# A decoder trunk with 31 instead of 28 slots for split weights, and 1 KB of descriptor region

## The chip, the core and the metric

The kernel runs on one core of a Trainium2 chip. TensorE (PE in the profile) multiplies, VectorE (DVE) and ScalarE (ACT) do elementwise work and copy results out of PSUM, GpSimd (POOL) does a few small operations, and SyncE (SP) issues the transfers between HBM and the on-chip memory SBUF. The metric is the device time of one execution in microseconds (us). Each engine takes its instructions in the order in which they stand in its program.

## What is computed

The reference is a decoder of four layers over 256 positions of width 1024, all in float32. Cut to its frame:

```python
def reference(x, ...):
    for i in range(DEPTH):                       # DEPTH = 4
        g = norm_g[i]
        x = x + 0.5 * rms_norm(swiglu(rms_norm(x, g[0]), ffn_w_in[i, 0], ffn_w_out[i, 0]), g[1])
        hm = rms_norm(x, g[2])
        # i % 3: 0 sliding_sink_attention, 1 nsa_attention, 2 moba_attention
        x = x + rms_norm(m, g[3])
        x = x + 0.5 * rms_norm(swiglu(rms_norm(x, g[4]), ffn_w_in[i, 1], ffn_w_out[i, 1]), g[5])
    return x
```

`swiglu` multiplies by a 1024 x 5632 and a 2816 x 1024 matrix; there are eight of them. The mixers of layers 0 and 3 attend to a window of 128 keys (called A below), that of layer 1 adds three branches with gates, one of them over compressed keys (B), and that of layer 2 is plain causal attention at this length (C).

## The kernel before

The 256 positions are two chains of 128 rows (`Chain`, t = 0 and 1), which pass through the same stages; at each step a recording layer takes the chain or side job that its own clock holds to be ready first (`choose`), so that one chain's matmuls fill the time in which the other's softmax or norm runs. What it takes is written into TensorE's program in that order, and the instructions of the other engines go into their programs as they come.

Weights come as 313 slabs of 128 x 2048 in two halves each, 625 halves in all (one slab is short). A half of 512 KB is loaded into one of four `raw` tiles, then split in two: ScalarE copies it to `hi` (rounded), VectorE subtracts to get `lo`. Both are tiles of 4 KB a partition in the pool `p4`, tag `k4`. Activations are split likewise into `xh` and `xl` (in the FFN's second product `hh` and `hl`), and each product is three matmuls: hi by xh, lo by xh, hi by xl. All matmul operands of this kind are 128 x 512; the groups of a half step (four contraction blocks) are 12 matmuls, called a proj group below.

The pool also holds the attention's keys (`kT`, `vs`, `cT`), queries, scores of chain 1, outputs `o`, and the compression's operands: everything that is 4 KB. How far the splitting runs ahead of TensorE is set by the free slots. Lines 366 and 387 count them:

```python
def room():
    return (SLOTS - 2 * (plan.split - plan.freed)
            - sum(max(h, w) for h, w in zip(plan.held, plan.want)))
...
        if plan.split < len(halves) and (urgent or clock.now >= plan.at + PACE) and room() >= 2:
            hi = p4.tile([P, HALF], F32R, tag="k4", name="hi")
            lo = p4.tile([P, HALF], F32R, tag="k4", name="lo")
```

`plan.freed` counts halves that both chains have used. So with 28 slots and nothing else held, 14 halves (seven slabs) are split at most. Where a `hi` stands in ScalarE's program is decided by this count and by the clock of the recording layer: it stands behind whatever was recorded before it, such as `h` (the gate of the FFN, read from a `proj` result) or `hh` (the copy of a transposed `h`).

In the setup, two of these slots hold a table for the position bias (`setup`, matmul `tab`), until it is written to `scratch`. In mixer B a side job (`compress`) adds position vectors to transposed keys (DVE `k<-k,post`, eight instructions), multiplies them (`hid`) and goes on to compressed keys and values, beside the two chains' scores (`acc<-k,k`), softmax, transposes (`trp`) and products with the values (`pv`). Transposes of keys and queries are `trq`.

Of the kernel before, what the change touches and what calls it, by code (L numbers as in the profile page):

```python
# [35 lines left out]

REP = 32
GATE_SLAB = 112
SLOTS = 28
NP2 = 6  # L40
NRAW = 4
NPP = 4
# [218 lines left out]
def trunk(ctx: ExitStack, tc: tile.TileContext, x, rel, gains, pre, sinks, pos, w1, w2, wts, hot,  # L261
# [5 lines left out]
    def pool(name, bufs, **kw):  # L267
        return ctx.enter_context(tc.tile_pool(name=name, bufs=bufs, **kw))

    const = pool("const", 1)  # L270
    praw = pool("praw", NRAW)
    p4 = pool("p4", SLOTS)
    p2 = pool("p2", NP2)
# [22 lines left out]
# [4 lines that stand above are left out]
    def k4(who, shape, dtype=F32):  # L300
        plan.held[who] += 1
        assert sum(plan.held) + 2 * (plan.split - plan.freed) <= SLOTS
        return p4.tile(shape, dtype, tag="k4", name="k4")
# [820 lines left out]
```

## Time and profile before

| | |
|---|---|
| median of 3 runs | 1977.15 us (1976.63 to 1980.09) |
| the profiled execution | 1981.12 us, its span 1979.3 us |
| TensorE busy | 1938.0 us, 98% of the span |
| VectorE, ScalarE busy | 1234.2 us (62%), 1039.2 us (53%) |
| mean granted clock of TensorE | 0.994 |

The span runs from the first to the last instruction; 1.8 us of the profiled execution lie outside it. Its time is 3.97 us above the median of the runs, within their spread. Busy times are unions of an engine's instructions; the ends of matmuls are modelled, so a matmul of 0.39 us that starts 0.23 us after the one before it overlaps it.

### The profile page before, as it was taken

The page shows a single profiled execution, that of the slowest core. Times are in us where ns is not written, and L with a number is a line of the kernel's source. Part 1 is how long each engine was busy: PE and PEld are TensorE (multiplying, and loading weights), DVE is VectorE, ACT ScalarE, POOL GpSimd, SP SyncE. Part 2 cuts the span into 40 slices and gives each one's busy share as a digit, 9 for nine tenths or more (in the row PEclk, how much of TensorE's full clock was granted, in tenths as well). Part 3 has the DMA queues.
Part 4 walks back from the last instruction along what each step waited for, and adds up shares of the span by engine and source line. Part 5 has one row for each costly group of instructions (what it writes and reads, how often), then busy time and mean ns, then how long its engine had stood idle before and what let it go on. Part 6 is the DMA issues. An engine that isn't in the chain of part 4 may idle for free.

```text
span 1979.3 us, 27414 instructions
## 1 busy us (share of the span) xinstructions
PE 1938.0 (98%) x9978; PEld 1586.7 (80%) x9978; DVE 1234.2 (62%) x2267; ACT 1039.2 (53%) x1885; POOL 43.0 (2%) x62
## 2 busy tenths in 40 slices
PE   7999999999999998999999999999999999999998
PEld 6778878888888876788888888778888888878887
DVE  6566666556655648765576556566557655676554
ACT  6345655445544546554455455655445544665442
POOL 0000000000000000000000000000000000000000
PEclk9999999999999999999999999999999999999999
DMA  8758556555556454465556555655555555436551
GB/s 271 210 192 241 176 137 200 190 185 186 195 188 193 153 165 116 139 202 188 185 170 209 185 185 175 188 148 196 185 189 181 195 188 191 161 112 205 185 186 58
DMA packets 114131, 356.42 MB, mean 180 GB/s; under 512 B 12843, under 2 KB 30507, under 8 KB 113996
## 3 DMA queue, kind: packets, MB, share of 16 engines
q1 hardware_dynamic: 113996, 354.68, 55.4%
q8 instruction: 78, 1.28, 0.3%
q14 instruction: 57, 0.47, 0.1%
HBM read 352.01 MB, written 2.62 MB: 179 GB/s over the span
## 4 chain that ended last, share of the span: by engine, by line
PE 90%; ACT 3%; DVE 3%; DMA 2%; issue 1%; SPq 0%; POOL 0%; DVEq 0%; POOLq 0%; ACTq 0%
PE proj L228 56%; PE acc L228 29%; ACT k L210 2%; PE trh L235 2%; DVE k L210 2%; DMA raw<-wts 1%; PE trx L235 1%; DVE lo L210 1%; PE pv L228 1%; DMA bias<-scratch 1%; PE trp L235 1%; ACT hi L210 1%; DVE pT L210 0%; PE trq L235 0%; ACT xh L210 0%
## 5 line engine op out<-in xcount | busy, mean ns | idle before, releaser
L210 DVE TENSOR_TENSOR lo<-raw,hi 128x1024 fp32r<-128x1024 f32 x625 | 760.3, 1223 | 371.3 <-ACT hi L210 338.7
L210 ACT ACTIVATE hi<-raw 128x1024 fp32r<-128x1024 f32 x625 | 659.3, 1063 | 369.3 <-PE acc L228 187.5
L228 PE MATMUL proj<-hi,xh 128*128 128x512 f32 (+1 forms) x1696 | 673.9, 398 | 2.7 <-DVE xl L210 1.7
L228 PE MATMUL proj<-lo,xh 128*128 128x512 f32 (+1 forms) x1696 | 657.4, 389 | 0.8 <-DVE lo L210 0.8
L228 PE MATMUL proj<-hi,xl 128*128 128x512 f32 (+1 forms) x1696 | 448.6, 387 | 0.0
L228 PEld LDWEIGHTS proj<-hi,xh 128*128 128x128 f32 x1696 | 320.0, 189 | 64.0 <-ACT xh L210 2.8
L228 PEld LDWEIGHTS proj<-lo,xh 128*128 128x128 f32 x1696 | 320.4, 189 | 61.4 <-DVE lo L210 1.1
L228 PEld LDWEIGHTS proj<-hi,xl 128*128 128x128 f32 x1696 | 315.6, 188 | 67.3
L228 PE MATMUL acc<-hi,hh 128*128 128x512 f32 x704 | 223.7, 392 | 3.1 <-ACT hh L210 3.1
L228 PE MATMUL acc<-lo,hh 128*128 128x512 f32 x704 | 222.2, 389 | 0.0
L228 PE MATMUL acc<-hi,hl 128*128 128x512 f32 x704 | 191.3, 390 | 0.0
L210 ACT ACTIVATE h<-proj,rh 128x256 f32<-128x256 f32 x176 | 81.9, 465 | 182.3 <-PE proj L228 180.8
L210 ACT ACTIVATE hh<-trh 128x256 fp32r<-128x256 f32 x176 | 67.0, 380 | 180.8 <-PE trh L235 180.7
L228 PEld LDWEIGHTS acc<-hi,hh 128*128 128x128 f32 x704 | 130.9, 188 | 30.2 <-ACT hh L210 3.9
L228 PEld LDWEIGHTS acc<-hi,hl 128*128 128x128 f32 x704 | 132.1, 188 | 27.7
L228 PEld LDWEIGHTS acc<-lo,hh 128*128 128x128 f32 x704 | 132.1, 188 | 27.6
L210 DVE SCALAR_TENSOR_TENSOR h<-h,proj 128x256 f32<-128x256 f32 x176 | 73.6, 418 | 116.2 <-ACT h L210 116.1
L210 DVE TENSOR_TENSOR hl<-trh,hh 128x256 fp32r<-128x256 f32 x176 | 73.9, 420 | 113.2 <-ACT hh L210 113.1
L210 DVE SCALAR_TENSOR_TENSOR h<-proj,c,h 128x256 f32<-128x256 f32 x176 | 85.0, 483 | 5.1
L210 ACT ACTIVATE k<-k,nm 128x128 f32<-128x128 f32 (+1 forms) x160 | 70.7, 445 | 32.0 <-DVE nm L210 32.0
L210 POOL TENSOR_TENSOR r<-v,mhalf 128x1 f32<-128x1 f32 x48 | 36.0, 750 | 1818.4 <-DVE v L210 1818.4
L235 PE MATMUL trh<-ident,h 128*128 128x128 f32 x352 | 67.0, 272 | 0.0
(99 smaller groups left out, 1133.4 us busy)
## 6 DMA issues: line engine op xcount, KB each, us to landing
raw<-wts SPq DMA_DIRECT2D x624, 512.0 KB, 4.6
bias<-scratch SPq DMA_DIRECT2D x96, 128.0 KB, 4.6
g<-gains SPq DMA_DIRECT2D x12, 512.0 KB, 4.8
k<-w SPq DMA_DIRECT2D x8, 512.0 KB, 8.3
scratch<-k SPq DMA_DIRECT2D x4, 384.0 KB, 6.6
out<-x SPq DMA_DIRECT2D x4, 256.0 KB, 2.0
x<-x SPq DMA_DIRECT2D x2, 256.0 KB, 3.0
x<-x SPq DMA_DIRECT2D x1, 512.0 KB, 7.2
```

Of the source, the lines that this page charges most:

```text
L210: return call(out, *args, **kw)
L228: self.engine.matmul(out, lhs, rhs, **kw)
L235: self.engine.transpose(out, src, ident)
```

## The change

Two constants. The pool of 4 KB tiles gets three slots more, 12 KB a partition, and the region that is set aside at the start of SBUF for descriptors of dynamic DMAs is set to 1024 bytes a partition; without the argument it has 16384.

```diff
-SLOTS = 28
+SLOTS = 31
@@ kernel()
-    nc = bacc.Bacc("TRN2", target_bir_lowering=False, num_devices=1)
+    nc = bacc.Bacc("TRN2", target_bir_lowering=False, num_devices=1,
+                   dynamic_dma_scratch_size=1024)
```

`SLOTS` also stands in `room()`, so the recording layer records splits earlier (with nothing else held 15 halves instead of 14), and since its clock decides by when a weight is ready, some instructions change places on every engine. The number of matmuls, 9262, stays. On TensorE all but some ten places read alike in both programs. Three places follow; numbers behind names tell tiles apart and are shifted between the two programs.

ScalarE, in the first FFN of layer 0, where the setup's two slots are held. Before, at the place where four splits follow an `h` that reads the finished `proj_900`:

```order
L210 ACTIVATE h_896<-proj_839,rh_257 128x256
L210 ACTIVATE hh_940<-trh_937 128x256
L210 ACTIVATE h_957<-proj_900,rh_290 128x256
L210 ACTIVATE hi_913<-raw_831 128x1024
L210 ACTIVATE hi_919<-raw_837 128x1024
L210 ACTIVATE hi_961<-raw_868 128x1024
```

Now, one block later (this place has splits ahead of its `hh` and `h` now):

```order
L210 ACTIVATE hh_1080<-trh_1077 128x256
L210 ACTIVATE h_1096<-proj_1040,rh_290 128x256
L210 ACTIVATE hi_1004<-raw_923 128x1024
L210 ACTIVATE hi_1010<-raw_929 128x1024
L210 ACTIVATE hi_1053<-raw_971 128x1024
...
L210 ACTIVATE hh_1218<-trh_1215 128x256
L210 ACTIVATE hi_1125<-raw_1057 128x1024
L210 ACTIVATE h_1234<-proj_1178,rh_290 128x256
L210 ACTIVATE hi_1143<-raw_1063 128x1024
```

So the burst of splits that stands behind an `h` has moved by one block of the FFN, and a second one follows: `hi_1143` stands behind `h_1234`.

TensorE at these places. Before, four matmuls stand between the end of `proj_900` and the first use of `hi_913`:

```order
L228 MATMUL proj_900<-hi_675,xl_231 128x512
L228 MATMUL proj_973<-hi_870,xh_126 128x512
L228 MATMUL proj_973<-lo_871,xh_126 128x512
L228 MATMUL proj_973<-hi_870,xh_128 128x512
L228 MATMUL proj_973<-lo_871,xh_128 128x512
L228 MATMUL proj_973<-hi_913,xh_130 128x512
L228 MATMUL proj_973<-lo_914,xh_130 128x512
```

Now none stands between `proj_1040` and `hi_1004`; at the second place there are again four, between `proj_1178` and `hi_1143`:

```order
L228 MATMUL proj_1040<-hi_772,xl_231 128x512
L228 MATMUL proj_1112<-hi_1004,xh_126 128x512
L228 MATMUL proj_1112<-lo_1005,xh_126 128x512
...
L228 MATMUL proj_1178<-hi_925,xl_231 128x512
L228 MATMUL proj_1250<-hi_1125,xh_126 128x512
L228 MATMUL proj_1250<-lo_1126,xh_126 128x512
L228 MATMUL proj_1250<-hi_1125,xh_128 128x512
L228 MATMUL proj_1250<-lo_1126,xh_128 128x512
L228 MATMUL proj_1250<-hi_1143,xh_130 128x512
L228 MATMUL proj_1250<-lo_1144,xh_130 128x512
```

TensorE where mixer B goes over from projections to scores. Before, ten transposes, three proj groups (cut here to the last matmul of one), four transposes, and then the first scores of chain 0 and of chain 1:

```order
L235 MATMUL trq_6562<-ident_94,k2_6493 128x128 x4
L235 MATMUL trq_6568<-ident_94,k2_6495 128x128 x4
L235 MATMUL trq_6574<-ident_94,k2_6547 128x128 x2
...
L228 MATMUL proj_6578<-hi_6556,xl_6242 128x512
L235 MATMUL trq_6674<-ident_94,k2_6638 128x128 x2
L235 MATMUL trq_6692<-ident_94,k2_6659 128x128 x2
L228 MATMUL acc_6685<-k4_6065,k4_6067 128x128 x2
L228 MATMUL acc_6686<-k4_6065,k4_6067 128x128 x2
L228 MATMUL acc_6703<-k4_6065,k4_6256 128x256 x2
L228 MATMUL acc_6704<-k4_6065,k4_6256 128x256 x2
```

Now the first proj group stands ahead of the transposes, the first scores of chain 0 right behind them, then two proj groups, and then three more groups of scores before `hid`:

```order
L235 MATMUL trq_6619<-ident_94,k2_6574 128x128 x2
L228 MATMUL acc_6600<-k4_6071,k4_6073 128x128 x2
L228 MATMUL acc_6601<-k4_6071,k4_6073 128x128 x2
...
L228 MATMUL proj_6640<-hi_6528,xl_6248 128x512
L228 MATMUL acc_6600<-k4_6071,k4_6073 128x128 x2
L228 MATMUL acc_6601<-k4_6071,k4_6073 128x128 x2
L235 MATMUL trp_6731<-ident_94,k2_6627 128x128 x2
L235 MATMUL trp_6736<-ident_94,k2_6627 128x128 x2
L235 MATMUL trq_6752<-ident_94,k2_6700 128x128 x2
L228 MATMUL acc_6763<-k4_6071,k4_6275 128x256 x2
L228 MATMUL acc_6764<-k4_6071,k4_6275 128x256 x2
```

So the first scores of chain 0 have moved ahead of two proj groups, and the transposes behind one. On VectorE the order there was: eight `post` additions, three `lo`, scores of chain 0, scores of chain 1. It is now: one `post`, the first scores of chain 0, seven `post`, two `lo`, the second scores of chain 0, one `lo`, the first scores of chain 1.

## Rows read from the trace of the kernel before

**Rows 1.** The page's head and its first part: busy us of each engine.
```profile
span 1979.3 us, 27414 instructions
PE 1938.0 (98%) x9978; PEld 1586.7 (80%) x9978; DVE 1234.2 (62%) x2267; ACT 1039.2 (53%) x1885; POOL 43.0 (2%) x62
```

**Rows 2.** Busy us by stretches of 100 us, then granted clock, DMA share.
```profile
0.00:100.00 100.00, 88.60 (x390) 71.39 (x391) 59.45 (x94) 51.48 (x79) 1.81 (x8) 1.00 0.76 238
...
500.00:600.00 100.00, 100.00 (x452) 82.26 (x451) 59.98 (x74) 48.08 (x61) 0.00 (x0) 1.00 0.60 199
...
700.00:800.00 100.00, 89.64 (x909) 70.89 (x907) 72.28 (x278) 59.95 (x184) 5.23 (x7) 0.97 0.45 138
```

**Rows 3.** Waits of PE over the span: us, times, longest.
```profile
PE trx L235 <- DMA x<-x: 8.4, 2, 4.7
PE acc L228 <- DVE mx L210: 5.4, 8, 1.6
...
PE proj L228 <- DVE lo L210: 0.8, 1, 0.8
...
PE proj L228 <- ACT hi L210: 0.6, 1, 0.6
```

**Rows 4.** Timeline of PE around 103 us: start, length, instruction, idle before.
```profile
102.04 0.39 PE L228 MATMUL proj<-hi,xh 128*128 128x512 f32 x1
...
102.72 0.39 PE L228 MATMUL proj<-lo,xh 128*128 128x512 f32 x1
103.72 0.50 PE L228 MATMUL proj<-hi,xh 128*128 128x512 f32 x1 [0.60 <-ACT hi L210]
104.98 0.50 PE L228 MATMUL proj<-lo,xh 128*128 128x512 f32 x1 [0.76 <-DVE lo L210]
```

**Rows 5.** Timeline of ACT, the same place.
```profile
102.24 0.47 ACT L210 ACTIVATE h<-proj,rh 128x256 f32<-128x256 f32 x1 [2.37 <-PE proj L228]
102.61 3.89 ACT L210 ACTIVATE hi<-raw 128x1024 fp32r<-128x1024 f32 x4
```

**Rows 6.** Busy us in three parts of mixer B, columns as in rows 2.
```profile
724.00:734.00 10.00, 9.49 (x43) 7.36 (x42) 9.29 (x10) 5.90 (x12) 0.00 (x0) 1.00 0.55 199
734.00:784.00 50.00, 41.58 (x538) 32.10 (x537) 42.78 (x210) 31.01 (x120) 3.78 (x5) 0.97 0.49 149
784.00:803.00 19.00, 17.42 (x232) 12.62 (x231) 15.49 (x57) 11.80 (x37) 2.56 (x3) 1.00 0.31 84
```

**Rows 7.** Timeline of PE at the start of mixer B's scores.
```profile
723.02 1.59 PE L235 MATMUL trq<-ident,k 128*128 128x128 f32 x10
...
733.68 0.44 PE L235 MATMUL trq<-ident,k 128*128 128x128 f32 x2 [0.35 <-ACT k L210]
...
739.26 0.72 PE L228 MATMUL acc<-k,k 64*128 64x128 f32 x8
739.91 0.66 PE L235 MATMUL trp<-ident,k 128*128 128x128 f32 x4
742.22 2.00 PE L228 MATMUL acc<-k,k 64*128 64x128 f32 x16 [1.65 <-DVE mx L210]
...
760.12 1.14 PE L228 MATMUL acc<-k,k 64*128 64x256 f32 x8
```

**Rows 8.** Timeline of DVE, the same place.
```profile
724.63 7.73 DVE L210 TENSOR_TENSOR k<-k,post 64x480 f32<-64x480 f32 x8 [4.68 <-ACT k L210]
732.39 3.50 DVE L210 TENSOR_TENSOR lo<-raw,hi 128x1024 fp32r<-128x1024 f32 x3
735.81 0.28 DVE L210 CUSTOM_DVE_ANT_0 k<-acc,bias 128x128 f32<-128x128 f32 x1
736.02 0.08 DVE L210 DVE_READ_ACCUMULATOR2_ANT mx<- 128x1 f32 x1
```

**Rows 9.** The page's DMA queue and its issues of weights: packets, MB; us to landing.
```profile
q1 hardware_dynamic: 113996, 354.68, 55.4%
...
raw<-wts SPq DMA_DIRECT2D x624, 512.0 KB, 4.6
```

## The prediction

> **What bounds the kernel now.** I read the page's busy times first, then the same by stretches, then TensorE's waits, and then timelines at the two places where the order of instructions changes. TensorE is busy for 1938.0 of 1979.3 us [rows 1], so all of its idle time is 41.3 us. The stretches show where that lies: in the FFNs there is none (100.00 of 100 us, at the full granted clock), in the first 100 us there are 11.4 us, in the stretch with mixer B 10.4 us [rows 2]. Of the first, 8.4 us are the wait for x itself [rows 3], which no slot touches. Two things follow. Splitting weights further ahead can give nothing inside the FFNs, where TensorE never waits. And a gain can only come from the places where TensorE starves: the setup and the mixers. Waits that name a weight (`lo` or `hi`) make 1.4 us in the whole run [rows 3]; the rest of the mixers' waits name the softmax, and there more weights help only if they let matmuls of a projection be put into the gaps.
>
> **The change part by part.** First the region of descriptors. All weight loads are issued from SyncE's queue, and the 113,996 packets of the run went through one queue that the page calls hardware_dynamic [rows 9]. No row shows the region used or not used, so its price is bounded from both sides. From below nothing: a transfer that doesn't read its descriptors there doesn't see its size. From above by the landing times: a weight load takes 4.6 us to land and four can be under way, so one lands every 1.15 us, while 625 halves in 1979.3 us are one every 3.17 us; a smaller region costs nothing until it makes a landing more than 2.7 times as long (12.7 us). I take nothing. The Trainium skill (DMA: Bandwidth & Descriptors, section "SWDGE vs HWDGE vs iDMA") says that the rings in SBUF belong to transfers that GpSimd issues and that those issued from SyncE or ScalarE never touch that path; by it the price is nothing as well, whatever the size, and no run before this one has a smaller region to show it.
>
> Then the three slots. They add no instruction: as many halves, matmuls and transfers as before. What changes is the order, at few places, so the cost is the sum over these.
>
> *The FFNs.* A split stands one half earlier there, and on ScalarE bursts of two and two become one and three. TensorE doesn't wait there and the order of its matmuls is the same, so the price is nothing as long as `hh` isn't held up. Its cover is a proj group: twelve matmuls at 0.227 us (102.04 to 102.72 is three of them [rows 4]) are 2.72 us. A burst of three is at most one split more ahead of an `hh`, 3.89 / 4 = 0.97 us [rows 5], less than the cover. If it were gone, eight FFNs of eleven blocks would each pay up to that, 85 us; nothing in the rows points to it.
>
> *The setup, around 103 us.* This is the place that I hold to be decisive. The setup's table takes two slots, no split is recorded for a while, and when they come they stand behind an `h` on ScalarE, which can't start before a `proj` is complete. Before, the rows show what this costs: `h` starts at 102.24, four `hi` follow from 102.61, and TensorE, which would have gone on at 102.72 + 0.23 = 102.95, starts at 103.72 with the first `hi`, 0.77 us late; its next matmul needs `lo`, starts at 104.98 instead of 103.95, and is 1.03 us late [rows 4, 5]. Sum 1.80 us, with four matmuls (102.04 to 102.72) between the end of `proj` and the first use of the new `hi`. In the changed program this place has its splits earlier, so the 1.80 us go. But one block later the same thing stands with no matmul between: TensorE would go on at the place of 102.04 and starts at that of 103.72, 1.68 us late, and 1.03 us for `lo` again, 2.71 us. And a block after that it stands once more with four matmuls between, as before: 1.80 us. So 4.51 us take the place of 1.80 us, a loss of 2.7 us. Behind the waiting matmul on TensorE everything waits; nothing makes it up, since the FFNs behind it run without a gap. From below this term is 0 (the splits could have run ahead by then for a reason that I don't see, such as a clock that is late on both sides), from above 4.5 us, if the old wait stayed too. I take 2.7 us.
>
> *Mixer B, 723 to 803 us.* Before, TensorE waits 0.35 and 1.65 us up to 742.22 [rows 7], and from 734 to 784 it is idle for 50 - 41.58 = 8.4 us in all [rows 6]. VectorE is the tighter engine there: busy 9.29 of 10 us from 724, and 42.78 of 50 us from 734 [rows 6]. In the changed program chain 0's first scores stand two proj groups ahead (5.44 us), which gives its softmax matmuls to hide behind. But the transposes that feed `compress` stand a proj group later, so VectorE's eight `post` additions start later. I go through the first part by rows. Transposes began at 723.02 and `post` at 724.63, 1.61 us behind [rows 7, 8]. Now the transposes begin at 723.02 + 2.72 = 725.74, two others stand ahead of those that matter (2 of 10 in 1.59 us, 0.3 us), so `post` starts at 727.65. VectorE then has eight `post` (7.73 us), the four score operations (0.21 us each from 735.81 to 736.02, 0.84 us), two `lo` of the three that took 3.50 us (2.33 us), to 738.6, and two score operations of the second job before the first PSUM bank is free: 739.0. TensorE: twelve transposes (1.9 us) to 727.65, scores 0.65 us (739.26 to 739.91), two proj groups 5.44, scores 0.65, four transposes 0.6, two more 0.3, scores over 256 keys 1.1 us (760.12), which is 736.4. It then needs that bank: a wait of 2.6 us. Before, the same part held 2.0 us of waits, so this is a loss of 0.6 us. At that point VectorE has done the same jobs in both programs, the remaining work is the same, and from 784 on the order of TensorE is the same again. What the middle, 744 to 784, does with its waits of 8.4 - 0.35 - 1.65 = 6.4 us is the open part: from below all of it goes (-6.4), from above VectorE's later start of 727.65 - 724.63 = 3.0 us is nowhere regained (+3.0). I take nothing for it, since VectorE's work there is the same and its share of 86% leaves little to shift.
>
> *Mixers A and C and the end.* In A the order of TensorE is the same; in C sixteen `pv` move behind the first products of the output projection, in the last A four transposes; each has matmuls of its own to stand beside. Nothing, give or take 0.6 us for the sixteen `pv` if the scores behind them are late.
>
> Sum: 2.7 + 0.6 = 3.3 us. The profiled execution took 1981.12 us and would take 1984.4; it is 3.97 us above the median of the runs, 1977.15 us, and against that the time is **1980.5 us**.
>
> **The rivals.** *The gaps of B are filled.* The earlier scores let the softmax of chain 0 run under proj groups, and the waits of 744 to 784 go, 6.4 us, with the 0.6 us of the first part not lost: 1977.15 + 2.7 - 6.4 = 1973.5 us, and with the old 2.0 us of the first part gone too, 1971.5 us. For it speaks that the waits there are many small ones; against it that VectorE is busy for 86% of that time and gets no work taken away. It ends as faster from a gain in B of 6.7 us on. *VectorE's late start in B is kept to the end.* Since `post` starts 3.0 us later and VectorE is nearly full behind it, all that follows is 3.0 us late: 1977.15 + 2.7 + 3.0 = 1982.9 us. For it speaks 9.29 of 10 us; against it 7.2 us of idle VectorE in the 50 us behind. It ends as slower where more than 1.3 us of the 3.0 stay. *The setup costs nothing.* The splits are on time, and the slots do what they do elsewhere, nothing: 1977.15 + 0.6 = 1977.8 us. The rows of 103 us speak against it. *The region throttles the loads.* With 1 KB for what had 16 KB, loads that could only go one at a time would land every 4.6 us, 625 of them in 2875 us; only a landing rate under one in 3.17 us decides. The single hardware queue speaks against it.
>
> **How the numbers follow.** A difference of 0.2%, 3.95 us, is about what a measurement of this kernel can tell from no change (the three runs spread over 3.46 us), so faster is below 1973.2 and slower above 1981.1 us. The forecast has a chance of 0.47, and its own terms move it by some 1.5 us to either side, so a fifth of it, 0.1, lies above 1981.1 us. The setup at no cost has 0.12 (same). B filled has 0.18, of which 0.12 get past 1973.2 us. B late has 0.22, of which 0.20 get past 1981.1 us. The throttled region has 0.01. That makes slower 0.31, same 0.57, faster 0.12. The range leaves out a tenth at each end: from 1974.0, inside B filled, to 1983.0, just above B late.
>
> **What the profile after would show.** TensorE's waits on `hi` and `lo` in the first 130 us: 0.60 and 0.76 us at 103 us should be gone, and in their place two pairs, about 1.7 and 1.0 us near 118 us and 0.8 and 1.0 us some 20 us later. In B the `post` additions should start 3 us later than before in relation to the last projections, with a wait of TensorE on `mx` of 2 to 3 us right ahead of `hid`. The FFNs should stay at 100.00 of 100 us. The landing of weights should stay near 4.6 us. I am wrong if the pairs in the setup don't appear, if the idle time in B changes by more than 3 us, or if any FFN shows waits.

## The result, and the profile after

The changed kernel took 1994.96 us (median of 4 runs, 1990.96 to 1997.79), the kernel before 1977.72 us (4 runs). The ratio is 1.0084, with an interval from 1.0064 to 1.0104. So it is slower, by 17 us in this comparison, and the prediction (1980.5 us, at most 1983.0) was wrong. Two later comparisons of the same two kernels, with 11 and 35 and with 11 and 31 runs, gave 1.0029 [1.0013, 1.0045] and 1.0034 [1.0016, 1.0052]: slower as well, by 6 to 7 us. Why the sizes differ is told below. One later run of each kernel took 9 and 15% longer, at a granted clock of 0.85 and 0.80, and is in no figure here.

The page of the changed kernel answers to [rows 1, 9]:

```profile
span 1993.9 us, 27323 instructions
...
PE 1942.3 (97%) x9978; PEld 1586.2 (80%) x9978; DVE 1230.1 (62%) x2267; ACT 1017.2 (51%) x1885; POOL 41.6 (2%) x62
...
q1 hardware_dynamic: 113996, 354.68, 56.2%
...
raw<-wts SPq DMA_DIRECT2D x624, 512.0 KB, 4.7
```

TensorE's idle time has grown from 41.3 to 51.6 us and its busy time by 4.3 us, though no matmul was added. Of the latter, 1.7 us are stretches at a lower clock (10.2 us were lost in them before, 11.9 us now, summed over windows of 5 us); the rest stays open. TensorE's waits over the span, against [rows 3]:

```profile
PE trx L235 <- DMA x<-x: 9.4, 2, 5.9
PE trx L235 <- DVE x L210: 7.2, 7, 2.2
PE acc L228 <- DVE mx L210: 6.9, 8, 2.9
PE acc L228 <- ACT hh L210: 3.7, 3, 2.5
PE proj L228 <- ACT hi L210: 2.1, 2, 1.5
...
PE pv L228 <- DVE v L210: 1.7, 1, 1.7
...
PE proj L228 <- DVE lo L210: 1.5, 2, 0.8
```

The row to see is the second. `trx` are the transposes of a chain's new x behind its norm, at the end of an FFN or mixer. Before they waited for x twice and 2.4 us, now seven times and 7.2 us. Of the 2.4 us, most is one wait behind the first mixer A,

```profile
273.61 1.94 PE L235 MATMUL trx<-ident,x 128*128 128x128 f32 x8 [1.98 <-DVE x L210]
```

which is 0.57 us now; without it the waits for x went from 0.4 to 6.6 us. The interior of the FFNs is as it was, 100.00 of 100 us, and the first 100 us have lost 2 us more than in [rows 2]:

```profile
0.00:100.00 100.00, 86.61 (x380) 69.89 (x381) 60.32 (x94) 52.03 (x79) 1.80 (x8) 1.00 0.77 241
500.00:600.00 100.00, 100.00 (x455) 82.35 (x453) 61.10 (x83) 47.38 (x68) 0.22 (x1) 1.00 0.60 192
```

**Where the time went.** I laid the two traces side by side at each `trx` and read how the distance grows. To the first: 1.0 us, the load of x, which another profile of the old order has too. In the first FFN with the setup: 6.4 us, of which 2.2 us are longer waits for `hi` and `lo` and 1.7 us a stretch at lower clock. In the first mixer A: -2.65 us, since 1.4 us of the wait just shown and a stretch at lower clock (0.85 at 270 and 0.81 at 275 us before) are missing. At the FFNs' later ends: 7.4 us in all, at most 2.2 us at one. In mixer B: -1.7 us, in C 0.3 us. In the last A: 3.8 us. The sum is 14.5 us.

**The end of an FFN.** ScalarE there, before and now (first the kernel before):

```profile
1003.05 1.06 ACT L210 ACTIVATE hi<-raw 128x1024 fp32r<-128x1024 f32 x1 [1.92 <-DMA raw<-wts]
1004.32 1.06 ACT L210 ACTIVATE hi<-raw 128x1024 fp32r<-128x1024 f32 x1 [0.21 <-DMA raw<-wts]
1005.29 0.58 ACT L210 ACTIVATE junk<-acc 128x512 bf16<-128x512 f32 x1
...
1006.03 0.60 ACT L210 ACTIVATE junk<-acc 128x512 bf16<-128x512 f32 x1
```

```profile
1008.70 1.06 ACT L210 ACTIVATE hi<-raw 128x1024 fp32r<-128x1024 f32 x1 [1.99 <-DMA raw<-wts]
1009.66 0.58 ACT L210 ACTIVATE junk<-acc 128x512 bf16<-128x512 f32 x1
...
1012.47 1.06 ACT L210 ACTIVATE hi<-raw 128x1024 fp32r<-128x1024 f32 x1 [2.14 <-DMA raw<-wts]
1013.44 0.58 ACT L210 ACTIVATE junk<-acc 128x512 bf16<-128x512 f32 x1
```

The two `junk` are the sums of squares of the two halves of the FFN's result; the norm, x and the next transposes wait for both. Now a `hi` stands between them, and it waits for its own load. VectorE and TensorE of the changed kernel show the rest of the chain:

```profile
1014.14 0.16 DVE L210 SCALAR_TENSOR_TENSOR v<-ss,v 128x1 f32<-128x1 f32 x1 [2.46 <-ACT junk L210]
...
1014.96 1.42 DVE L210 SCALAR_TENSOR_TENSOR x<-k,r,x 128x512 f32<-128x512 f32 x2
```

```profile
1015.86 1.23 PE L235 MATMUL trx<-ident,x 128*128 128x128 f32 x8 [2.23 <-DVE x L210]
```

That `hi` was recorded behind the `junk` (tiles are numbered as they are recorded) and still stands ahead of the second one, because the order in the programs of ScalarE, VectorE and SyncE isn't that of the recording: the compiler moves instructions against each other. The section on the kernel said otherwise (a `hi` "stands behind whatever was recorded before it"). ScalarE's program at this norm in the changed kernel:

```
L210 ACTIVATE junk_99,ss_9442<-acc_7958 128x512
L210 ACTIVATE hi_9479<-raw_9397 128x1024
L210 ACTIVATE junk_99,ss_9442<-acc_7959 128x512
```

In the program before, where the same `hi` stands behind both, the norms of an FFN's or mixer's result have a `hi` between their two `junk` at 8 places, all of chain 1; now at 16. Seven of the eight new places are in chain 0.

**Why there.** A slab of two halves gives its four slots back in the order lo, lo, hi, hi, as TensorE is done with them, and new halves take slots in the order in which they come free. By the slots in the compiled programs, with 28 slots 272 of the 625 halves take two former `lo` and 270 two former `hi`. With 31 the row is shifted by one: 269 take a former `lo` for their `hi` and a former `hi` for their `lo`, and 267 take the last `hi` of one slab for their `hi` and the first `lo` of the next for their `lo`. Every second `lo` therefore waits until the next slab is in use, and so does the load into the raw tile that this `lo` sets free. VectorE's waits, first before, then now:

```profile
DVE lo L210 <- ACT hi L210: 338.7, 337, 12.1
...
DVE lo L210 <- PE acc L228: 7.6, 3, 4.4
```

```profile
DVE lo L210 <- ACT hi L210: 178.7, 206, 12.1
...
DVE lo L210 <- PE acc L228: 87.6, 65, 2.3
...
DVE lo L210 <- PE trh L235: 41.3, 58, 0.8
```

`lo` behind its own `hi` became `lo` behind TensorE, 123 times. That an odd number of slots does this was the first theory ("pairs"); its rivals were the changed order of TensorE, which comes with the higher count in `room()` ("order"), and the descriptor region.

### The profile page after: what moved, and what is told of

It reads as the page before. It is cut to its first block, busy times and chain, and to the rows that moved or that the text cites. A ratio compares the mean times of both kernels' runs of the same rounds, so it can differ in the third digit from the quotient of the medians.

```text
span 1993.9 us, 27323 instructions
## 1 busy us (share of the span) xinstructions
PE 1942.3 (97%) x9978; PEld 1586.2 (80%) x9978; DVE 1230.1 (62%) x2267; ACT 1017.2 (51%) x1885; POOL 41.6 (2%) x62
## 4 chain that ended last, share of the span: by engine, by line
PE 85%; DMA 5%; DVE 5%; ACT 4%; issue 2%; POOL 0%; SPq 0%; DVEq 0%; POOLq 0%; ACTq 0%
PE proj L228 53%; PE acc L228 27%; DMA raw<-wts 4%; ACT k L210 2%; PE trh L235 2%; DVE k L210 2%; DVE lo L210 1%; PE trx L235 1%; ACT hi L210 1%; DMA bias<-scratch 1%; PE pv L228 1%; ACT junk L210 1%; DVE x L210 0%; PE trp L235 0%; DVE pT L210 0%
## 5 line engine op out<-in xcount | busy, mean ns | idle before, releaser
L210 ACT ACTIVATE hi<-raw 128x1024 fp32r<-128x1024 f32 x625 | 646.2, 1060 | 479.7 <-PE acc L228 192.5
```

The source lines that it names most:

```text
L210: return call(out, *args, **kw)
```

## The experiments

In the table, "counted" is the number that `room()` works with, "slots" that of the pool. The kernel before was run beside each four on the same chip: medians 1982.33, 1982.72, 1982.83 and 1982.04 us. Each run is listed with its mean granted clock, and time times clock, called the product here, is an estimate of what the run would have taken at full clock: the waits are in it, what a lower clock costs is not. It is the sharper measure: the runs of before (126) have a standard deviation of 3.1 to 4.0 us in time and of 1.4 to 1.6 us in this product, whose means on the four chips are 1972.0, 1971.7, 1971.9 and 1971.4. The last column is the mean product against that of before on the same chip; its standard error is 0.4 to 0.9 us.

| run | slots, counted | median us | ratio, interval | mean clock | product |
|---|---|---|---|---|---|
| e1_region | 28, 28 | 1983.63 | 0.9993 [0.998, 1.0007] | 0.9951 | 0.0 |
| e2_31_counted_28 | 31, 28 | 1987.48 | 1.003 [1.0016, 1.0043] | 0.9947 | +5.8 |
| e3_30 | 30, 30 | 1990.29 | 1.0039 [1.0025, 1.0052] | 0.9938 | +5.7 |
| e4_29 | 29, 29 | 1987.51 | 1.0039 [1.0019, 1.0059] | 0.9964 | +10.5 |
| e5_32_counted_31 | 32, 31 | 1987.31 | 1.0023 [1.0011, 1.0035] | 0.9948 | +5.6 |
| e6_setup_28 | 32, 28 in the setup | 1983.44 | 1.0005 [0.9991, 1.0018] | 0.9953 | +2.0 |
| e7_end_28 | 32, 28 in layer 3 | 1987.04 | 1.0023 [1.0012, 1.0033] | 0.9938 | +3.3 |
| e8_mid_31 | 32, 28 in both | 1980.38 | 0.9986 [0.9975, 0.9996] | 0.9958 | +0.2 |
| e9_31_again | 31, 31 | 1988.90 | 1.0029 [1.0013, 1.0045] | 0.9950 | +7.1 |
| e10_31_junk_first | 31, 31 | 1984.01 | 1.0005 [0.999, 1.002] | 0.9949 | +1.8 |
| e11_31_counted_28_junk_first | 31, 28 | 1983.71 | 1.0002 [0.9987, 1.0017] | 0.9934 | -1.1 |
| e12_mid_31_junk_first | 32, 28 in both | 1982.79 | 1.0008 [0.9991, 1.0025] | 0.9940 | -0.5 |
| e13_set_31 | 32, 31 in the setup | 1991.92 | 1.0058 [1.0037, 1.0079] | 0.9930 | +7.6 |
| e14_end_31 | 32, 31 in layer 3 | 1988.26 | 1.0031 [1.0016, 1.0047] | 0.9949 | +6.0 |
| e15_32_counted_28 | 32, 28 | 1983.25 | 1.0004 [0.9988, 1.0021] | 0.9951 | +2.8 |
| e16_31_third | 31, 31 | 1988.96 | 1.0034 [1.0016, 1.0052] | 0.9955 | +8.6 |

All of them have the 1 KB region.

**Region, odd pool, order (e1 to e4).** The edits, against the changed kernel: `SLOTS` is 28, 30 or 29 in e1, e3 and e4; e2 is

```diff
-SLOTS = 31
+SLOTS, COUNT = 31, 28
-        return (SLOTS - 2 * (plan.split - plan.freed)
+        return (COUNT - 2 * (plan.split - plan.freed)
-        assert sum(plan.held) + 2 * (plan.split - plan.freed) <= SLOTS
+        assert sum(plan.held) + 2 * (plan.split - plan.freed) <= COUNT
```

e1: 

> 28 slots as before, and only the descriptor region is 1 KB; every engine has the order of before. Region theory (the smaller region slows transfers): all or most of the loss is here, about 1995 us, and the landing of weights is the 4.7 us of the changed kernel or more. Pairs theory (an odd number of slots parts hi and lo of one half) and order theory (the recording layer's earlier splits change the order): no difference, 1977.7 us, ratio between 0.998 and 1.002.

e2: 

> The pool has 31 slots, but the recording layer counts 28, so TensorE's order is that of before to the last instruction; only the order on ScalarE, VectorE and SyncE changes. Pairs theory: a hi still stands between the two junk of chain 0's norms, so the loss at the ends of the FFNs (about 7.4 us) and that of the last mixer A (about 4 us) stay and only the setup's part goes: about 1989 us, with trx waiting for x some seven times. Order theory: nothing in TensorE's order has changed, so 1977.7 us and two waits for x as before.

e3: 

> 30 slots, counted as 30: an even number, with two of the three slots more and a changed order of TensorE. Pairs theory: hi and lo stay together, no hi between the two junk of chain 0, trx waits for x twice as before, and what is left is the setup's order: 1977.7 to 1981 us. Order theory: two thirds of the loss of 17 us, about 1989 us.

e4: 

> 29 slots, counted as 29: an odd number, with one of the three slots more, and TensorE's order nearly that of before. Pairs theory: hi and lo are parted, the losses at the ends of the FFNs and in the last mixer A are there in full: about 1989 to 1992 us, some seven waits of trx for x. Order theory: a third of the loss or none, at most 1983 us.

e1 is the kernel before in time and product, with weights landing in 4.6 us: the region costs nothing. The Trainium skill (DMA: Bandwidth & Descriptors, section "SWDGE vs HWDGE vs iDMA") says that transfers issued from SyncE never touch those rings, and the run agrees. e2 has TensorE's order of before and is slower all the same, e3 has an even pool and is slower too. So neither pairs nor order alone is the cause; both theories fall in their pure form. TensorE's waits for x, first in e2, then in e3:

```profile
PE trx L235 <- DVE x L210: 7.7, 7, 2.9
```

```profile
PE trx L235 <- DVE x L210: 4.1, 6, 2.0
...
PE proj L228 <- ACT hi L210: 2.1, 2, 1.5
PE proj L228 <- DVE lo L210: 1.5, 2, 0.8
```

The odd pool has the waits at the norms and not those of the setup, the even one the other way round, but for its six waits for x, where two were forecast. Their count alone doesn't tell the pools apart: e1, with the order of before, has five. Without the wait behind the first mixer A they come to 0.4 us in before, 1.4 in e1 and 2.1 in e3, and with odd pools to 4.9 in e2, 5.1 in e4, 6.6 in the changed kernel and 4.3 and 3.0 in its later profiles (e9, e16). VectorE's `lo` waited for `acc` 66 times and 89.8 us in e2, and three times, 7.6 us, in e3. e4, with one slot more and odd, has the odd pool's waits and the last A's, as expected; that its product is the highest of all, at the best clock, I can't explain: its profile shows 6.0 us more idle time than before, not 10.5.

**The count's parts (e5 to e8).** The pool has 32 slots, so pairs are whole, and TensorE's order in e5 is that of the changed kernel; the parts are taken away by (the lines with + are e5, e6, e7 and e8, one each)

```diff
-SLOTS = 31
+SLOTS = 32
-        return (SLOTS - 2 * (plan.split - plan.freed)
+        return (31 - 2 * (plan.split - plan.freed)
+        return ((31 if 66 < plan.split else 28) - 2 * (plan.split - plan.freed)
+        return ((31 if plan.split < 475 else 28) - 2 * (plan.split - plan.freed)
+        return ((31 if 66 < plan.split < 475 else 28) - 2 * (plan.split - plan.freed)
```

e5: 

> A pool of 32 slots counted as 31: TensorE has the order of the changed kernel to the last instruction, only the pool is even. Two-cause theory (the parting of hi and lo by an odd pool costs about 6 us at the ends of the FFNs, the count of 31 costs about 5 us in the setup and 4 us in the last mixer A): the 6 us go and the rest stays, 8 to 10 us slower than before, waits of trx for x at most five with 4 us in all. If the order alone made the whole loss: 16 us slower, as the changed kernel. If the odd pool made it all: no difference from before.

e6: 

> As the kernel with 32 slots counted as 31, but the first 67 halves are counted with 28, so ScalarE's order in the setup is that of before. Theory (two pairs of waits and a window at half clock in the setup, 5.3 us in the profiles): 3 to 5 us faster than the kernel with 32 counted as 31, that is 4 to 6 us slower than before; the waits for hi and lo at 122 and 144 us are gone and those of 103 us are back. Rival (the setup's loss is in how the run began and not in the order): no difference from the kernel with 32 counted as 31.

e7: 

> As the kernel with 32 slots counted as 31, but from half 475 on (layer 3) counted with 28, so the four transposes of the last mixer A stand ahead of the output projection again. Theory (pT behind the norm on VectorE, 2 us, and a further window at half clock, 1.7 us): 3 to 4 us faster than the kernel with 32 counted as 31; pv waits for v no more. Rival (the last A's loss belongs to the late weights or the clock and not to the transposes): no difference.

e8: 

> 32 slots, counted as 31 for halves 67 to 474 and as 28 before and behind them, so that the setup and the last mixer A have the order of before and only mixers B, C and the FFNs between keep the new one. If the three causes (odd pool, setup, last A) are the whole loss: no slower than before, and by the gain of 1.5 to 2.9 us that the profiles show in mixer B, 0 to 3 us faster. If a part of the loss has another cause: still 3 us or more slower.

e5 lies below its expected 8 to 10 us (4.6 by medians, 5.6 by product). Taking the setup's order away gives 3.9 us by medians (3.6 by product), as expected. For the last A 3 to 4 us were expected, and the medians contradict each other (0.3 us from e5 to e7, 3.1 us from e6 to e8), the products don't: 2.3 and 1.9 us. With both away the kernel is 2.3 us faster than before, as expected, and by product equal to it.

**The `hi` between the `junk` (e9 to e12).** e9 is the changed kernel; the rule of the others is

```diff
+    norm_last = [None]
-                nc.scalar.activation(junk, src[k], AF.Square, accum_out=ss[:, k:k + 1])
+                norm_last[0] = nc.scalar.activation(junk, src[k], AF.Square, accum_out=ss[:, k:k + 1])
-            nc.scalar.activation(hi[:, :n], r[:, :n], AF.Copy)
+            with tc.issue_after(norm_last[0].ins) if norm_last[0] else ExitStack():
+                nc.scalar.activation(hi[:, :n], r[:, :n], AF.Copy)
```

e9: 

> The changed kernel once more, beside the three below, since so far it was timed in few runs. If the odd pool (6 us with 31 counted as 28) and the count of 31 (4.6 us with 32 slots) only add up: 10 to 11 us slower than before, ratio 1.0054. If the two make each other worse: 14 to 17 us, ratio 1.007 to 1.0084.

e10: 

> The changed kernel with one more rule for ScalarE: a hi that is recorded behind a norm's two junk is issued behind them. TensorE's order stays that of the changed kernel. Theory (the odd pool costs by the hi between the two junk, which waits for its load): what is left is the count's part, 4 to 6 us slower than before, at most five waits of trx for x with 4 us in all, as with 32 slots counted as 31. Rival (the odd pool costs by lo and by late loads everywhere, not at the norm): no faster than the changed kernel, 10 us or more slower than before.

e11: 

> 31 slots counted as 28 with the same rule, so that TensorE's order is that of before and hi and lo are parted by the odd pool, but no hi stands between two junk. Theory: the 6 us of the kernel without the rule go, within 2 us of before. Rival: they stay, 5 to 7 us slower than before.

e12: 

> 32 slots, counted as 31 for halves 67 to 474 and 28 elsewhere, with the rule that no hi stands between two junk. Before has eight such places too, all in norms of chain 1 and of no visible cost. Theory: as without the rule, 2 to 3 us faster than before, and up to 1 us more if the last waits of trx for x (2.6 us) shrink. Rival (splits held back behind the norm come late): slower than without the rule, no better than before.

e10 leaves TensorE's order and the odd pool as they are (`lo` still waits for `acc` 61 times, 85.9 us) and only sends a `hi` behind the norm. It takes 4.9 us off e9 (5.3 by product), and e11, each against before on its own chip, 4.3 us off e2 (6.9 by product). So the odd pool's price is paid at the norm and hardly anywhere else. But the rule takes away more than this price. It also sends back every `hi` that was recorded behind a norm and stood ahead of its first `junk`, of which even pools have some too (in the program before, at 22 of 48 norms). So e10 is only 1.2 us slower than before (1.8 by product), below its expected 4 to 6 us and below e5, the even pool with the same count. The odd pool alone is e9 and e16 against e5, 1.5 and 3.0 us by product (other chips), and e2 against e15 and before, which count 28 too, 3.0 and 5.8 us. An even pool with the rule was run only as e12. TensorE's waits in e10:

```profile
PE proj L228 <- ACT hi L210: 2.1, 2, 1.5
...
PE pv L228 <- DVE v L210: 1.7, 1, 1.7
...
PE proj L228 <- DVE lo L210: 1.5, 2, 0.8
...
PE trx L235 <- DVE x L210: 1.0, 2, 0.6
```

The waits for x are down to 1.0 us, less than before has; those of the setup and of the last A, which the rule doesn't touch, are there. e12 brought next to nothing beside e8 (-0.7 us by product) and ran at a lower clock: it is not the 2 to 3 us faster than before that were expected, and inconclusive. e9's ratio is below what adding the two causes gave (1.0054).

**One part alone (e13 to e16).** As e5, with `31 if plan.split < 67 else 28` (e13), `28 if plan.split < 475 else 31` (e14) and `28` (e15); e16 is the changed kernel.

e13: 

> 32 slots, counted as 31 only for the first 67 halves and as 28 behind them: TensorE's order is that of before, ScalarE's splits in the setup stand as in the changed kernel. Theory (the setup's order costs 3.5 to 5 us of the count's part): 3 to 5 us slower than the kernel with 32 counted as 28 everywhere; waits for hi and lo of 2.1 and 1.5 us near 122 and 144 us. Rival (the setup's loss only came with the rest of the count): within 1.5 us of it.

e14: 

> 32 slots, counted as 28 up to half 474 and as 31 from there: TensorE's order differs from that of before only in the last mixer A, where four transposes stand behind the output projection. Theory (pT behind the norm on VectorE makes waits of 2 us, and a window at half clock may come with them): 2 to 4 us slower than the kernel with 32 counted as 28 everywhere. Rival, after the run that took this part away alone and was no faster: within 1.5 us of it.

e15: 

> 32 slots counted as 28 everywhere: the base for the two above. The pool is even and TensorE's order is that of before. Theory: as before, ratio 0.9985 to 1.0015. If physical slots beyond the count cost or give anything by themselves: outside of that.

e16: 

> The changed kernel a third time. First it took 16.6 us more than before, then 6.0 us (means). The profile of the first had weights landing in 4.7 us and 7.2 us of waits of trx for x, that of the second 4.4 us and 4.9 us. If the size of the loss follows the landing: with 4.4 us again 5 to 8 us slower, with 4.7 us more than 10 us slower. If it does not: any size with either landing.

Against e15, the setup's order alone costs 8.7 us by medians and 4.8 by product, the last A's 5.0 and 3.2; the medians are above the expected ranges, the products within. Their waits, of e13 and of e14:

```profile
PE proj L228 <- ACT hi L210: 2.1, 2, 1.5
```

```profile
PE pv L228 <- DVE v L210: 1.7, 1, 1.7
```

So the last A's order does cost something. e16 is in the range expected for a landing of 4.4 us, which it has; but two runs of the same landing don't show that the size follows it.

**The size of the first comparison.** The changed kernel's four runs were all listed at a clock of 0.993, a product of 1980.7 us, which is 0.7 to 1.8 us above those of e9 and e16 (1978.9, 1980.0). So by product its waits were little longer than later (its profile is idle for 51.6 us, theirs for 45.6 and 46.1), and at their clock of 0.995 it would have taken some 4 us less. The four runs of before in that comparison have no clock listed; at its product of 1971.8 us their 1977.72 us mean 0.997 (an estimate), against 0.9946 later, another 5 us. By these numbers the loss is 7 to 9 us of waits, and the clock of few runs made 17 of it.

## Why the prediction was wrong

*What bounds the kernel, and the region:* right. The loss is in the setup, the last mixer and the norms, where TensorE starves; e1 is no different from before.

*The FFNs*, the step that failed: "the price is nothing as long as `hh` isn't held up". `hh` wasn't, and the FFNs' interiors show no wait. But at an FFN's end the path leads over `junk`, and I had looked at ScalarE's bursts only for what stands ahead of `hh`. The argument that a split "stands one half earlier" missed that with an odd pool `hi` and `lo` part, so that loads come later and not earlier. Measured, in place of 0: an odd pool costs 1.5 to 3.0 us at the changed kernel's count and 3.0 to 5.8 us at a count of 28, by product, and the rule that keeps a `hi` behind the norm takes all of it away (5.3 and 6.9 us).

*The setup:* the mechanism and the waits were right, and the clock was left out. The waits at 103 us are gone, and two pairs stand near where they were forecast. The first, with 1.51 and 0.76 us of idle time, is late by the 1.68 and 1.03 us that were forecast (four matmuls of 0.227 us from 119.87 on last until 120.78 us, and the next starts at 122.46; the one behind it could start at 122.69 and starts at 123.72):

```profile
119.87 1.08 PE L228 MATMUL proj<-hi,xl 128*128 128x512 f32 x4
122.46 0.50 PE L228 MATMUL proj<-hi,xh 128*128 128x512 f32 x1 [1.51 <-ACT hi L210]
123.72 0.50 PE L228 MATMUL proj<-lo,xh 128*128 128x512 f32 x1 [0.76 <-DVE lo L210]
...
143.78 0.50 PE L228 MATMUL proj<-hi,xh 128*128 128x512 f32 x1 [0.58 <-ACT hi L210]
145.04 0.50 PE L228 MATMUL proj<-lo,xh 128*128 128x512 f32 x1 [0.76 <-DVE lo L210]
```

By product, from which the clock is taken out, the term measured 3.1 to 4.8 us (e7 to e8, e5 to e6, e15 to e13, with standard errors of 0.6 to 1.0 us), a little above the 2.7 us of the sum. By medians it is 3.9 to 8.7 us. What the sum left out is the clock behind the first pair, here in two windows with the columns of [rows 2]:

```profile
120.00:125.00 5.00, 2.73 (x10) 1.49 (x9) 3.47 (x5) 4.01 (x5) 0.00 (x0) 0.94 0.04 8
125.00:130.00 5.00, 5.00 (x17) 4.00 (x17) 3.06 (x3) 1.31 (x2) 0.00 (x0) 0.72 0.88 269
```

From 124.62 to 126.33 matmuls start every 0.43 us instead of 0.23, which is 1.2 GHz and not 2.4; 5 us at 0.94 and 5 at 0.72 lose 1.7 us. Seven of the eight profiles with these two pairs have such a stretch there, and none of the other ten.

*Mixer B:* the wait of 2.6 us ahead of `hid` came (2.92 us on `mx` at 743.03). For the open part, taken as nothing, a gain is not shown: waits that name the softmax and the compression went from 10.2 us in the 86 us of B to 8.5, but e1, with the order of before, has 8.5 us too. By product, e8 is 2.6 us below e15, which differs from it by the count in the middle layers alone. But part of that is e15's own: in B it waits 1.8 us for `xh` and `xl`, before 0.2 us. Against before, e8 is 2.3 us faster by medians and by product equal. So of the 6.4 us of the rival "gaps of B are filled", 0 to 2.6 came. (Two readings of [rows 6] in the prediction were off: of the 8.4 us behind 734 the wait of 0.35 us should not have been taken, since it ends at 733.68, which leaves 6.8 us and not 6.4; and from 724 to 734 VectorE, at 9.29 us, is not busier than TensorE, at 9.49.) VectorE kept little: its last `post` addition ended 1.6 us later against the start of B, not 3.0 us.

*The last A* was the second term wrongly put at nothing: "four transposes; each has matmuls of its own to stand beside. Nothing". They do, but VectorE's copy of their result now stands behind chain 0's norm:

```profile
1782.93 1.42 DVE L210 SCALAR_TENSOR_TENSOR x<-k,r,x 128x512 f32<-128x512 f32 x2
1784.26 0.68 DVE L210 COPY pT<-trp 128x512 f32<-128x512 f32 x1
```

```profile
1782.62 0.69 PE L228 MATMUL pv<-k,pT 128*64 128x64 f32 x16 [0.45 <-ACT pT L210]
1785.00 0.69 PE L228 MATMUL pv<-k,pT 128*64 128x64 f32 x16 [1.70 <-DVE v L210]
```

Before, the copy ran ahead of the norm's second half, and `pv` waited 0.17 us:

```profile
1769.48 0.69 DVE L210 COPY pT<-trp 128x512 f32<-128x512 f32 x1 [0.33 <-PE trp L235]
```

```profile
1770.22 0.69 PE L228 MATMUL pv<-k,pT 128*64 128x64 f32 x16 [0.17 <-DVE pT L210]
```

The price is 1.9 to 3.2 us by product. (The row names `v`; what `pv` needs is the copy right ahead of it.)

In sum, by product against before: the middle layers 0.2 us (e8), the setup 3.1 to 3.6 and the last A 1.9 to 2.3 on top of them, together 5.6 in e5; and the odd pool 1.5 and 3.0 more, which makes the 7.1 and 8.6 us of e9 and e16. What stays open: e4's 10.5 us, and why e15, 32 slots counted as 28, is 2.8 us above before by product. Its profile shows two places: 0.9 us more behind the first mixer A (2.86 us for 1.98) and the 1.6 us more in mixer B for `xh` and `xl`; e13 and e14, with the same count there, wait at both places too.

## What to carry to other kernels

Where two tiles of one step come from one rotating pool, change its size by whole steps: an odd size parts the pair, and the later half holds back the next load. When instructions that run ahead are moved, look at each short chain that shares their engine (here the norm's two sums), not only at the one that the inner loop waits for, and order it explicitly where the compiler may put a waiting instruction into it. And compare runs by time times granted clock as well as by time: it halved the scatter here and settled what medians left in contradiction. It doesn't replace the time, since what a change costs in clock, as in the setup here, isn't in it.

## What the runs showed of the hardware that was not expected

The scatter of this kernel's times is for the most part clock. In all 18 profiles, span less TensorE's idle time (39.9 to 51.6 us) less what stretches below full clock lost (6.5 to 16.1 us, summed over whole windows of 5 us) is 1927.8 to 1932.6 us, whatever the order. These stretches lie at a few places, and not in every run. Most are in or right behind a wait of TensorE, but not those near 680 and 710 us. In e9, TensorE had no gap from 670 us on; it ran 24 narrow products (128x48) from 677.38 and eight transposes from 680.06 us, and then matmuls every 0.43 us until 683.5:

```profile
675.00:680.00 5.00, 5.00 (x40) 4.67 (x38) 3.12 (x7) 3.84 (x10) 0.55 (x1) 1.00 0.12 27
680.00:685.00 5.00, 5.00 (x21) 4.25 (x22) 4.61 (x14) 5.00 (x15) 0.35 (x1) 0.66 0.73 250
```

The changed kernel at 740 to 745 us had a granted clock of 0.50 in e9 and 0.85 in e16, with the same program.

```profile
740.00:745.00 5.00, 5.00 (x24) 2.73 (x25) 3.85 (x29) 3.72 (x16) 0.00 (x0) 0.50 0.89 247
```

```profile
740.00:745.00 5.00, 3.46 (x24) 2.51 (x26) 5.00 (x24) 1.38 (x7) 0.00 (x0) 0.85 0.71 218
```

In e9 TensorE had been busy for 2.05 of the 5 us before (735 to 740), in e16 for 3.58.
